# Sixty one-number memsets on VectorE ahead of gamma's copy, in a grouped instance norm

## The chip, the cores and the metric

The kernel runs on one core of one Trainium2 chip. The metric is the device time of one execution, in microseconds (us). Before the change three runs gave 626.84, 627.01 and 627.31 us, a median of 627.01 us.

## The reference

x has the shape 4 x 8 x 16 x 256 x 256 in float32, 134 MB; gamma has 8 x 16 numbers. Each of the 512 channels (4 x 8 x 16) is normed over its 65,536 pixels and multiplied by its gamma:

```python
mu = x.mean(axis=(3, 4), keepdims=True)
var = ((x - mu) ** 2).mean(axis=(3, 4), keepdims=True)
x_norm = (x - mu) / np.sqrt(var + 1e-5)
out = x_norm * gamma[None, :, :, None, None]
```

So 134 MB are read and 134 MB are written.

## The kernel before

A unit is 16 channels. Each channel is spread over S = 8 partitions, so a unit is a tile of 128 partitions x 8192 numbers, 4.19 MB, and there are U = 32 units. Six slots (AHEAD = 6) hold units; unit u uses slot u % 6 and is normed in place.

The order of the work is the order in which the program is written, engine by engine (the schedule is manual): each engine goes through its own instructions in order, and waits for another engine or for a transfer only where the data demand it.

*Setup.* VectorE clears a small tile, touch (L53). POOL's queue then writes touch over 16 short stretches of the first unit's output (L54), which the first unit's store later overwrites, and loads gamma into g_row, one row of 128 numbers (L55). The first six units are loaded at once, units 1 and 3 from ScalarE's queue, the others from SP's (the helper at L48). POOL makes eps_t, one and navg, a 128 x 128 matrix that holds -1/65536 where two partitions belong to one channel (L61 to L70). VectorE waits for gamma and copies it into g_rep with each number repeated 8 times (L81); TensorE turns the row into columns with one small matmul for each of the 8 groups of 16 channels (L86), and VectorE copies the result to g_col (L92).

*The loop over 32 units.* VectorE sums the tile (L105) while ScalarE squares and sums it (L106). TensorE adds these sums over the 8 partitions of each channel (L114). VectorE makes the negative variance (L115), ScalarE the root (L119), VectorE the reciprocal (L123) and its product with g_col (L125), then VectorE norms the tile in place (L128). ScalarE's queue stores it (L132), and SP's queue loads unit u + 6 into the same slot (L48), once that store has landed.

Three things set the order around the change. VectorE's first instructions are touch's memset, gamma's copy, g_col's copy and the first reduction, in that order. POOL's first transfer waits for touch's memset. Gamma's copy waits for gamma's transfer.

Of the kernel before, what the change touches and what calls it, by code (L numbers as in the profile page):

```python
# [1 line left out]

# [4 lines left out]

F32 = mybir.dt.float32
U8 = mybir.dt.uint8
ALU = mybir.AluOpType  # L10
ACTF = mybir.ActivationFunctionType
AX = mybir.AxisListType


@with_exitstack
def kernel(
    ctx: ExitStack,
    tc: tile.TileContext,
    x: bass.AP,
    gamma: bass.AP,  # L20
    out: bass.AP,
):
    nc = tc.nc
    B, G, C, H, W = x.shape
    P = nc.NUM_PARTITIONS
    HW = H * W
    n_ch = B * G * C
    S = 8
    K = P // S
    F = HW // S  # L30
    U = n_ch // K
    NG = (G * C) // K
    AHEAD = 6
    assert HW % S == 0 and (G * C) % K == 0

    xv = x.rearrange("b g c h w -> (b g c h w)").rearrange("(u p f) -> u p f", p=P, f=F)
    ov = out.rearrange("b g c h w -> (b g c h w)").rearrange("(u p f) -> u p f", p=P, f=F)
    gv = gamma.rearrange("g c -> (g c)")

    data = ctx.enter_context(tc.tile_pool(name="data", bufs=1))  # L40
    singles = ctx.enter_context(tc.tile_pool(name="singles", bufs=1))
    psum = ctx.enter_context(tc.tile_pool(name="psum", bufs=4, space=bass.MemoryType.PSUM))
    ctx.enter_context(tc.manual_schedule())

    slots = [data.tile([P, F], F32, name=f"xt{i}") for i in range(AHEAD)]

    def load(u, queue):
        queue.dma_start(out=slots[u % AHEAD][:], in_=xv[u])  # L48


    g_row = singles.tile([1, G * C], F32, name="g_row")
    touch = singles.tile([16, 128], F32, name="touch")
    nc.vector.memset(touch[:], 0.0)  # L53
    nc.gpsimd.dma_start(out=ov[0][0::S, 0:128], in_=touch[:])  # L54
    nc.gpsimd.dma_start(out=g_row[:], in_=gv[None, :])  # L55
    for u in range(AHEAD):
        load(u, nc.scalar if u in (1, 3) else nc.sync)


    eps_t = singles.tile([P, 1], F32, name="eps_t")  # L60
    nc.gpsimd.memset(eps_t[:], 1e-5)  # L61
    one = singles.tile([1, 1], F32, name="one")
    nc.gpsimd.memset(one[:], 1.0)
    navg = singles.tile([P, K, S], F32, name="navg")
    nc.gpsimd.memset(navg[:], -1.0 / HW)  # L65
    nc.gpsimd.affine_select(  # L66
        out=navg[:], in_=navg[:], pattern=[[-S, K], [0, S]], compare_op=ALU.is_ge,
        fill=0.0, base=0, channel_multiplier=1,
    )
    nc.gpsimd.affine_select(  # L70
        out=navg[:], in_=navg[:], pattern=[[S, K], [0, S]], compare_op=ALU.is_ge,
        fill=0.0, base=S - 1, channel_multiplier=-1,
    )
    navg_w = navg[:].rearrange("p k s -> p (k s)")
    root_eps = singles.tile([P, 1], F32, name="root_eps")
    nc.scalar.activation(out=root_eps[:], in_=eps_t[:], func=ACTF.Sqrt)  # L76
    g_rep = singles.tile([1, NG, K, S], F32, name="g_rep")
    g_ps = psum.tile([P, NG], F32, name="g_ps", bufs=1)
    g_col = singles.tile([P, NG], F32, name="g_col")

    nc.vector.tensor_copy(  # L81
        out=g_rep[:],
        in_=g_row[:].rearrange("o (n k) -> o n k", n=NG).unsqueeze(3).to_broadcast([1, NG, K, S]),
    )
    for n in range(NG):
        nc.tensor.matmul(  # L86
            out=g_ps[:, n : n + 1],
            lhsT=g_rep[:, n].rearrange("o k s -> o (k s)"),
            rhs=one[:],
            start=True, stop=True,  # L90
        )
    nc.vector.tensor_copy(out=g_col[:], in_=g_ps[:])  # L92

    junk = singles.tile([P, F], U8, name="junk")

    st = singles.tile([P, U, 2], F32, name="st")
    nvar = singles.tile([P, U], F32, name="nvar")
    std = singles.tile([P, U], F32, name="std")
    rstd = singles.tile([P, U], F32, name="rstd")
    scale = singles.tile([P, U], F32, name="scale")  # L100

    squares = []
    for u in range(U):
        t = slots[u % AHEAD]
        nc.vector.reduce_sum(out=st[:, u, 0:1], in_=t[:], axis=AX.X)  # L105
        square = nc.scalar.activation(  # L106
            out=junk[:], in_=t[:], func=ACTF.Square, accum_out=st[:, u, 1:2],
        )
        if u:

            tc.declare_no_dep(square.ins, squares[-1].ins, reason="junk, ordered by the root between")
        squares.append(square)
        ps = psum.tile([P, 2], F32, name="ps")
        nc.tensor.matmul(out=ps[:], lhsT=navg_w, rhs=st[:, u], start=True, stop=True)  # L114
        nc.vector.tensor_scalar(  # L115
            out=nvar[:, u : u + 1], in0=ps[:, 0:1], scalar1=ps[:, 0:1],
            scalar2=ps[:, 1:2], op0=ALU.mult, op1=ALU.add,
        )
        nc.scalar.activation(  # L119
            out=std[:, u : u + 1], in_=nvar[:, u : u + 1], func=ACTF.Sqrt,  # L120
            bias=eps_t[:], scale=-1.0,
        )
        nc.vector.reciprocal(out=rstd[:, u : u + 1], in_=std[:, u : u + 1])  # L123
        g = u % NG
        nc.vector.tensor_mul(  # L125
            out=scale[:, u : u + 1], in0=rstd[:, u : u + 1], in1=g_col[:, g : g + 1],
        )
        nc.vector.tensor_scalar(  # L128
            out=t[:], in0=t[:], scalar1=ps[:, 0:1], scalar2=scale[:, u : u + 1],
            op0=ALU.add, op1=ALU.mult,  # L130
        )
        nc.scalar.dma_start(out=ov[u], in_=t[:])  # L132
        if u + AHEAD < U:
            load(u + AHEAD, nc.sync)


# [1 line left out]
_INS = ['x', 'gamma']  # L138
_OUTS = [((4, 8, 16, 256, 256), 'float32')]


# [23 lines left out]
```

## Time and profile before

| what | value |
|---|---|
| median of three runs | 627.01 us |
| span of the profiled execution, first to last instruction | 625.4 us |
| median less span | 1.6 us |
| bytes moved by DMA | 268.46 MB, mean 429 GB/s |
| VectorE (DVE) busy | 443.4 us, 71% of the span |
| ScalarE (ACT) busy | 238.8 us, 38% |
| granted TensorE clock | 1.000 |
| touch's transfer, issue to landing | 9.1 us |
| gamma's transfer, issue to landing | 13.3 us |
| a load of x on SP's queue, median, issue to landing | 38.5 us |
| a store, median, issue to landing | 62.5 us |

The profile is of one execution; it gives its span and no other time of it, so the median of the unprofiled runs is set beside the span. Engines appear as PE (TensorE matmul), PEld (its weight loads), DVE (VectorE), ACT (ScalarE), POOL (GpSimd) and SP; a q behind the name is the engine's queue, which waits and issues DMAs. A group of instructions has the line, the engine, the operation, out<-in, the shapes and the count, then the busy time in us and the mean of one in ns, then the idle time of the engine just before and what ended it. The slices are 40 equal parts of the span (15.6 us each), a digit is the busy share in tenths, and GB/s is what the DMA engines moved. A load or store takes long from issue to landing where it stands in a queue with others.

### The profile page before, as it was taken

To read this page: it belongs to the slowest core of one execution; us is meant where nothing else is said; L and a number is where in the kernel's file an instruction comes from. 1 tells how busy PE (TensorE), PEld (TensorE's weight loads), DVE (VectorE), ACT (ScalarE), POOL (GpSimd) and SP (SyncE) were. 2 spreads that over 40 slices of the span, in tenths; PEclk is the share of its full clock that TensorE was granted. 3 is DMA by queue.
4 is the path that set the end of the run, shared out by engine and by line. 5 is a ranking of instruction groups with operands and counts; after the bars stand their busy time and mean duration, and the time that the engine had idled before them with its cause. 6 is when DMAs were issued, how large, how long until landed. Compare 5 with 4: busy or idle time off the path is not lost.

```text
span 625.4 us, 631 instructions
## 1 busy us (share of the span) xinstructions
PE 21.4 (3%) x80; PEld 19.5 (3%) x80; DVE 443.4 (71%) x163; ACT 238.8 (38%) x98; POOL 2.4 (0%) x11
## 2 busy tenths in 40 slices
PE   0200000000000000000000000000000000000000
PEld 0200000000000000000000000000000000000000
DVE  0588999999776687666776767867668676686730
ACT  0444444444443244432344423444224442244400
POOL 1000000000000000000000000000000000000000
DMA  8999999999999999999999999999999999999998
GB/s 369 436 402 436 436 436 436 436 434 424 434 436 432 432 428 434 436 436 436 436 434 423 434 436 432 436 428 434 434 436 436 436 436 432 425 434 434 434 432 363
DMA packets 9282, 268.46 MB, mean 429 GB/s; under 512 B 1072, under 2 KB 1088, under 8 KB 1088
## 3 DMA queue, kind: packets, MB, share of 16 engines
q10 hardware_dynamic: 4896, 142.61, 52.9%
q1 hardware_dynamic: 4320, 125.83, 46.7%
q0 software_dynamic: 64, 0.01, 0.0%
q14 instruction: 2, 0.02, 0.0%
HBM read 134.22 MB, written 134.23 MB: 429 GB/s over the span
## 4 chain that ended last, share of the span: by engine, by line
another core or an unknown queue 61%; DMA 17%; DVE 15%; SPq 1%; PE 1%; issue 0%; ACT 0%
DVE st L105 10%; DMA xt<-in_x_dram 10%; DMA out_dram<-xt 8%; DVE xt L128 5%; SPq L48 1%; PE ps L114 1%; ACT std L119 0%; DVE nvar L115 0%; DVE rstd L123 0%; DVE scale L125 0%
## 5 line engine op out<-in xcount | busy, mean ns | idle before, releaser
L105 DVE TENSOR_REDUCE st<-xt 128x1 f32<-128x8192 f32 x32 | 277.9, 8685 | 100.8 <-DMA xt<-in_x_dram 100.8
L106 ACT ACTIVATE junk<-xt 128x8192 uint8<-128x8192 f32 x32 | 225.0, 7030 | 275.6 <-DMA xt<-in_x_dram 232.4
L128 DVE TENSOR_SCALAR xt<-xt,ps,scale 128x8192 f32<-128x8192 f32 x32 | 145.6, 4551 | 1.2
L119 ACT ACTIVATE std<-nvar,eps_t 128x1 f32<-128x1 f32 x32 | 9.4, 295 | 79.6 <-DVE nvar L115 79.6
L114 PE MATMUL ps<-st,navg 128*128 128x2 f32 x64 | 17.8, 348 | 557.6 <-DVE st L105 557.6
L114 PEld LDWEIGHTS ps<-st,navg 128*128 128x128 f32 x64 | 16.0, 311 | 559.4 <-issue 559.4
L115 DVE TENSOR_SCALAR nvar<-ps 128x1 f32<-128x1 f32 x32 | 9.2, 288 | 23.8 <-PE ps L114 23.8
L123 DVE RECIPROCAL rstd<-std 128x1 f32<-128x1 f32 x32 | 5.3, 164 | 11.6 <-ACT std L119 11.6
L81 DVE COPY g_rep<-g_row 1x1024 f32<-1x1024 f32 x1 | 0.7, 681 | 14.2 <-DMA g_row<-in_gamma_dram 14.2
L106 ACT ACTIVATION_READ_ACCUMULATOR junk<-xt 128x1 f32 x32 | 6.0, 187 | 0.0
L125 DVE TENSOR_TENSOR scale<-rstd,g_col 128x1 f32<-128x1 f32 x32 | 5.1, 160 | 1.1
L86 PE MATMUL g_ps<-one,g_rep 1*128 1x1 f32 x16 | 3.5, 347 | 16.1 <-DVE g_rep L81 16.1
L86 PEld LDWEIGHTS g_ps<-one,g_rep 1*128 1x128 f32 x16 | 3.5, 326 | 16.1 <-issue 16.1
L92 DVE COPY g_col<-g_ps 128x8 f32<-128x8 f32 x1 | 0.2, 167 | 3.7 <-PE g_ps L86 3.7
L76 ACT ACT_TABLE_LOAD x1 | 1.3, 1283 | 1.7 <-PEq L149 1.7
L53 DVE MEMSET touch<- 16x128 f32 x1 | 0.2, 165 | 0.9 <-PEq L149 0.9
L54 POOL DMA_DIRECT2D out_dram<-touch x1 | 0.6, 617 | 0.8 <-DVE touch L53 0.8
L55 POOL DMA_DIRECT2D g_row<-in_gamma_dram x1 | 0.5, 484 | 0.0
L66 POOL TENSOR_SCALAR_AFFINE_SELECT navg<-navg 128x128 f32<-128x128 f32 x1 | 0.4, 398 | 0.1
L70 POOL TENSOR_SCALAR_AFFINE_SELECT navg<-navg 128x128 f32<-128x128 f32 x1 | 0.4, 397 | 0.1
L65 POOL MEMSET navg<- 128x128 f32 x1 | 0.2, 231 | 0.0
L76 ACT ACTIVATE root_eps<-eps_t 128x1 f32<-128x1 f32 x1 | 0.2, 203 | 0.0
(6 smaller groups left out, 0.6 us busy)
## 6 DMA issues: line engine op xcount, KB each, us to landing
out_dram<-xt ACTq DMA_DIRECT2D x32, 4096.0 KB, 62.5
xt<-in_x_dram SPq DMA_DIRECT2D x30, 4096.0 KB, 38.5
xt<-in_x_dram ACTq DMA_DIRECT2D x2, 4096.0 KB, 31.7
out_dram<-touch POOLq DMA_DIRECT2D x1, 8.0 KB, 9.1
g_row<-in_gamma_dram POOLq DMA_DIRECT2D x1, 0.5 KB, 13.3
```

Source lines behind the costliest of these rows:

```text
L48: queue.dma_start(out=slots[u % AHEAD][:], in_=xv[u])
L76: nc.scalar.activation(out=root_eps[:], in_=eps_t[:], func=ACTF.Sqrt)
L81: nc.vector.tensor_copy(out=g_rep[:], in_=g_row[:].rearrange("o (n k) -> o n k", n=NG).unsqueeze(3).to_broadcast([1, NG, K, S]),)
L86: nc.tensor.matmul(out=g_ps[:, n : n + 1], lhsT=g_rep[:, n].rearrange("o k s -> o (k s)"), rhs=one[:], start=True, stop=True,)
L105: nc.vector.reduce_sum(out=st[:, u, 0:1], in_=t[:], axis=AX.X)
L106: square = nc.scalar.activation(out=junk[:], in_=t[:], func=ACTF.Square, accum_out=st[:, u, 1:2],)
L114: nc.tensor.matmul(out=ps[:], lhsT=navg_w, rhs=st[:, u], start=True, stop=True)
L115: nc.vector.tensor_scalar(out=nvar[:, u : u + 1], in0=ps[:, 0:1], scalar1=ps[:, 0:1], scalar2=ps[:, 1:2], op0=ALU.mult, op1=ALU.add,)
L119: nc.scalar.activation(out=std[:, u : u + 1], in_=nvar[:, u : u + 1], func=ACTF.Sqrt, bias=eps_t[:], scale=-1.0,)
L123: nc.vector.reciprocal(out=rstd[:, u : u + 1], in_=std[:, u : u + 1])
L125: nc.vector.tensor_mul(out=scale[:, u : u + 1], in0=rstd[:, u : u + 1], in1=g_col[:, g : g + 1],)
L128: nc.vector.tensor_scalar(out=t[:], in0=t[:], scalar1=ps[:, 0:1], scalar2=scale[:, u : u + 1], op0=ALU.add, op1=ALU.mult,)
```

## The change

Behind the issue of the first six loads in the program's text, a new tile of 64 numbers on one partition is made, and VectorE clears its first 60 numbers one by one. Nothing reads the tile. On VectorE these instructions come behind touch's memset and ahead of gamma's copy.

```diff
     for u in range(AHEAD):
         load(u, nc.scalar if u in (1, 3) else nc.sync)
 
+    spare = singles.tile([1, 64], F32, name="spare")
+    for i in range(60):
+        nc.vector.memset(spare[:, i : i + 1], 0.0)
 
     eps_t = singles.tile([P, 1], F32, name="eps_t")
     nc.gpsimd.memset(eps_t[:], 1e-5)
```

## The prediction

> **What bounds the kernel now.** I read the page from the top: the busy shares first, then the slices, because a share is only a mean. VectorE (DVE) has the largest share, yet the two last lines of the slices carry the verdict.
>
> ```profile
> PE 21.4 (3%) x80; PEld 19.5 (3%) x80; DVE 443.4 (71%) x163; ACT 238.8 (38%) x98; POOL 2.4 (0%) x11
> ...
> DVE  0588999999776687666776767867668676686730
> ...
> DMA  8999999999999999999999999999999999999998
> GB/s 369 436 402 436 436 436 436 436 434 424 434 436 432 432 428 434 436 436 436 436 434 423 434 436 432 436 428 434 434 436 436 436 436 432 425 434 434 434 432 363
> ...
> q14 instruction: 2, 0.02, 0.0%
> ...
> L105 DVE TENSOR_REDUCE st<-xt 128x1 f32<-128x8192 f32 x32 | 277.9, 8685 | 100.8 <-DMA xt<-in_x_dram 100.8
> ```
>
> The DMA row is at 8 or 9 tenths from the first slice to the last, and the rate hardly leaves 436 GB/s. The table of stretches gives 433 GB/s between 100 and 500 us. At that rate the page's 268.46 MB take 268.46 / 0.433 = 620.0 us of a span of 625.4. So the DMA engines bound the kernel, and only a change that lets them run dry, or adds bytes, can move the end by much. VectorE stands idle for 100.8 us in front of its reductions, in wait for loads: it is the faster partner in the steady part.
>
> Next the start, in the timeline of instructions (start, duration, engine, line, in brackets the idle time before).
>
> ```profile
> 0.34 0.10 POOL L149 MEMSET const-float32-1.0<- 128x1 f32 x1
> 0.38 0.10 POOL L149 MEMSET const-bfloat16-1.0<- 128x1 bf16 x1
> ...
> 0.89 0.17 DVE L53 MEMSET touch<- 16x128 f32 x1 [0.89 <-PEq L149]
> 1.36 0.62 POOL L54 DMA_DIRECT2D out_dram<-touch  x1 [0.85 <-DVE touch L53]
> ...
> 1.98 0.48 POOL L55 DMA_DIRECT2D g_row<-in_gamma_dram  x1
> ...
> 15.29 0.68 DVE L81 COPY g_rep<-g_row 1x1024 f32<-1x1024 f32 x1 [14.23 <-DMA g_row<-in_gamma_dram]
> ...
> 19.70 0.17 DVE L92 COPY g_col<-g_ps 128x8 f32<-128x8 f32 x1 [3.73 <-PE g_ps L86]
> ...
> 22.57 8.69 DVE L105 TENSOR_REDUCE st<-xt 128x1 f32<-128x8192 f32 x1 [2.71 <-DMA xt<-in_x_dram]
> ...
> 33.05 4.55 DVE L128 TENSOR_SCALAR xt<-xt,ps,scale 128x8192 f32<-128x8192 f32 x1
> 37.51 8.68 DVE L105 TENSOR_REDUCE st<-xt 128x1 f32<-128x8192 f32 x1
> 37.63 0.35 ACTq L132 DMA_DIRECT2D out_dram<-xt  x1
> ```
>
> The place of the change is the 14.23 us between touch's memset (ends at 1.06) and gamma's copy at 15.29. VectorE does nothing there; it waits for gamma's transfer. Behind it lies a second reserve: g_col is ready at 19.87 (19.70 + 0.17), and the first reduction starts only at 22.57, when the first unit of x has landed, 2.71 us later. The chain that ended last agrees: its first piece is that load, from 0.81 to 22.55, and neither gamma nor touch is in it.
>
> Last the end, in the waits of SP's queue (total us, times, longest us).
>
> ```profile
> SPq L160 <- DMA out_dram<-xt: 38.4, 4, 9.6
> ```
>
> After the last load SP waits for four stores one behind the other, 38.4 / 4 = 9.6 us each. A store of 4.19 MB at 433 GB/s is 9.7 us. The last store is issued at 600.80 and lands 23.6 us later: 14 us of that it stands behind stores issued before it. The end is a draining queue, and compute could be some 14 us later there at no cost.
>
> **The change, step by step.** Nothing is removed. 60 memsets of one number each are added to VectorE, behind touch's memset (L53) and ahead of gamma's copy (L81). The tile is new and nobody reads it, so no engine waits for them; touch's memset stays first, and POOL's transfer at L54, which waits for it, is released as before. No DMA is added or moved on any queue.
>
> *The pace of a memset.* No row shows such a memset, so I bound it. From below: POOL's small memsets start 0.03 us apart (0.34, 0.38) though each lasts 0.10; 60 x 0.03 = 1.8 us. From above: each memset waits for the end of the one before, if the framework orders writes to one tile. The row for that is the reciprocal at 32.65 and the multiplication behind it at 32.85, which needs its result: 0.20 us from start to start; 60 x 0.20 = 12.0 us. I take a value between: VectorE's own memset of a wider tile lasts 0.165 us, and two independent VectorE instructions overlap by 0.09 us (the one at 33.05 ends at 37.60, the next begins at 37.51), which leaves 0.075 us a piece, 4.5 us in all.
>
> The sum: 1.06 + 4.5 = 5.6 us, and at the upper end 1.06 + 12.0 = 13.1 us. Both are ahead of 15.29, so gamma's copy starts when it did, and the cost is nothing. The cover is gamma's transfer; it is gone from (15.29 - 1.06) / 60 = 0.237 us a memset. Beyond that the 2.71 us in front of the first reduction still hide the delay, up to (14.23 + 2.71) / 60 = 0.282 us.
>
> The Trainium skill, Perfetto Trace Analysis, section Optimizing Scalar/DVE Operations, gives about 60 ns of engine time for a VectorE access to SBUF, and a profiled length of about twice that. By it 60 memsets would be an estimated 3.6 us, and the sum would be the same nothing.
>
> *POOL beside them.* POOL writes touch's and gamma's descriptors from 1.36 to 2.46, now beside the memsets. From below that costs nothing, and it can gain nothing, since the first of them still waits for touch's memset. From above, the memsets shut POOL out until the last has ended, at 13.1: touch's issue moves from 1.36 to 13.1, 11.7 us, and gamma's copy with it to 27.0. g_col ends 4.58 us after the copy starts (19.87 - 15.29), so at 31.6; the first reduction, queued behind it on VectorE, starts 31.6 - 22.57 = 9.0 us late, and the first store at 46.6 instead of 37.63. I take nothing, since POOL's row of 0.62 us for the issue and VectorE's one-partition write of four bytes show no reason for more.
>
> A rule speaks against this change: the Trainium skill, SBUF — State Buffer, section SBUF: two separate sides, warns that a DMA issued from GpSimd is held up while VectorE runs an operation in a mode that uses two ports. Its section Who interferes with whom says that a VectorE instruction with at most one SBUF input outside those modes does not contend. No run here shows either; by the first the sum would hold a late gamma, by the second nothing.
>
> *Code.* 60 more instructions have to be loaded. The page shows two instruction packets in the whole span, 0.02 MB; the trace has them at 156 and 200 us, 8 KB and 0.31 us each. One more would cost one of the 16 DMA engines 0.31 us. Whether VectorE would stop for it, no row shows. From above I take gamma's transfer, also small and also among the loads: 13.3 us from issue to landing. With the dearest memsets, VectorE would then reach the copy at 1.06 + 12.0 + 13.3 = 26.4, and the first store would be 26.4 + 4.58 - 22.57 = 8.4 us late, at 46.0. I take 0 and keep 0.31 us for the range.
>
> *What a late first store costs.* This is the step that makes the upper ends harmless. Six loads are issued at once, 25.17 MB, 58.1 us at 433 GB/s. The first two land at 22.5, and they are 19.4 us of transfer, so the stream begins at 3.1 and lasts to 61.2 without any store. The first store adds 9.7 us: 70.9. When it lands, SP issues the seventh load; the second store follows the first by 14.9 us, VectorE's period (37.51 - 22.57). So the engines run dry only if the second store is issued later than 70.9, which puts the first later than 56.0, that is over 18.4 us late. Both upper ends above, 46.6 and 46.0, are well short of that. In the steady part VectorE needs 14.9 us a unit and the transfers 8.39 MB / 0.433 = 19.4 us, so a lateness of 9 us is made up within three units.
>
> The sum of the change against the profiled span is therefore 625.4 + 0 = 625.4 us. The median of the runs, 627.01, lies 1.6 us above that span; the change has no part in that rest, so the forecast is 627.0 us.
>
> **The rivals.**
>
> *The first store moves, the end hardly.* POOL held up or a stop for code, as above, with the first store 8 to 9 us late. For it: small transfers among the loads take 13.3 us here. Against it: the writes are tiny and the cover is 14 us. The bytes stay the same, only the mixing of loads and stores changes. Between 36 and 48 us, where the first store meets the loads, the stretches show 401, 385 and 393 GB/s: (3 x 433 - 1179) x 4 / 433 = 1.1 us lost. This could be lost again or saved: 625.9 to 628.1 us, within 0.2% at both ends.
>
> *Slower.* The memsets hold up VectorE so long that the engines run dry. Place: between the loads' end at 61.2 and the seventh load. It decides from a first store 18.4 us late, which takes (22.57 + 18.4 - 4.58 - 1.06) / 60 = 0.59 us a memset. The only short hop in the profile that dear is from VectorE through PE and back, 0.74 us idle ahead of L115. At that price the first store starts 1.06 + 44.4 + 4.58 - 22.57 = 27.5 us late, at 65.1; the engines stand 3.9 us after 61.2, and once more for the restart, which by the table of stretches lost about 2.3 us between 0 and 6 us of the span. That is 6.2 us: 633.2 us. Against it: these memsets wait for no other engine.
>
> *The change does not do what it says.* The memsets might be dropped or merged on the way to the chip, since nobody reads them. The time would be 627.0 us as well; only the profile could tell it from the forecast.
>
> **How the numbers follow.** The forecast, memsets hidden under gamma's transfer, 0.88; the memsets not there, 0.01; the first store late, 0.06; slower through a dry queue, 0.03; the remaining 0.02 is for a gain that I can't name. A difference of 0.2% (1.25 us) is about what a measurement of this kernel can tell from no change. Within it: 0.88 + 0.01 + 0.05 of the late store = 0.94. Slower: 0.03 + 0.01 of the late store = 0.04. Faster: 0.02. The range: the three runs of before reach from 626.84 to 627.31, 0.47 wide; as much again on each side is 626.37 to 627.78, and 0.31 for one instruction packet makes the upper end 628.1. So 626.3 to 628.1 us, which also takes in the upper half of the late store.
>
> **What would show it right or wrong.** Right: 60 memsets between 1.06 and at most 13.1 us, copy of g_rep at about 15.3 with a wait for gamma still ahead of it (some 10 us), first reduction at about 22.6, first store at about 37.6, slices as before. A copy at 27 with POOL's issues late says that POOL was shut out; memsets with a hole in their row say code. If the first store is in its place and the time still moves by over 1.25 us, the reasoning from the queues is wrong.

## The result and the profile after

The changed kernel took 629.72 us (median of 7 runs, 628.17 to 631.45) beside 626.87 us before: a ratio of 1.0045, 95% interval 1.0033 to 1.0057. It is slower by 2.8 us and outside the range of the prediction. Repeated three times later it had ratios of 1.0028 to 1.0030, and medians 1.4 to 1.7 us above those of before, again outside the range. The profiled execution has a span of 626.6 us instead of 625.4.

The page of the changed kernel, slices, queues and the new group:

```profile
DVE  1598999999776687666786767857678676686730
...
DMA  8999999999999999999999999999999999999997
GB/s 369 433 416 433 423 435 435 435 435 435 435 435 436 427 429 431 435 435 431 435 435 435 425 435 435 436 433 435 435 435 433 429 427 431 435 435 435 435 435 326
...
q14 instruction: 3, 0.02, 0.0%
...
L61 DVE MEMSET spare<- 1x1 f32 x60 | 1.6, 59 | 0.0
```

The mean rate is as high as before in the middle and lower in the last slice, 326 GB/s instead of 363. There is one more instruction packet. The memsets take 1.6 us together.

The start in its timeline (start, duration, engine, line, idle time before):

```profile
1.00 1.61 DVE L61 MEMSET spare<- 1x1 f32 x60
1.36 0.62 POOL L54 DMA_DIRECT2D out_dram<-touch  x1 [0.85 <-DVE touch L53]
...
1.97 0.48 POOL L55 DMA_DIRECT2D g_row<-in_gamma_dram  x1
...
16.07 0.68 DVE L84 COPY g_rep<-g_row 1x1024 f32<-1x1024 f32 x1 [13.46 <-DMA g_row<-in_gamma_dram]
...
23.36 8.69 DVE L108 TENSOR_REDUCE st<-xt 128x1 f32<-128x8192 f32 x1 [2.72 <-DMA xt<-in_x_dram]
...
38.42 0.35 ACTq L135 DMA_DIRECT2D out_dram<-xt  x1
```

The memsets end at 2.61, and VectorE then still waits 13.46 us for gamma: the cover is as wide as predicted. POOL issues its two transfers when it did. Yet gamma, the first load and the first store are all 0.8 us late. The time of the memsets is not the reason; the transfers themselves take longer (touch's 9.8 us from issue to landing instead of 9.1, gamma's 14.1 instead of 13.3).

Where the end moved is seen in the table of stretches, between 624.00 and 625.20 us (length, busy time of each engine, clock, DMA share, GB/s), of the kernel before:

```profile
624.00:625.20 1.20, 0.00 (x0) 0.00 (x0) 0.00 (x0) 0.00 (x0) 0.00 (x0) 1.00 0.00 0
```

and of the changed kernel:

```profile
624.00:625.20 1.20, 0.00 (x0) 0.00 (x0) 0.00 (x0) 0.00 (x0) 0.00 (x0) 1.00 0.06 27
```

A share of 0.06 is one of 16 engines, and 27 GB/s over 1.2 us is one packet of 32,768 bytes; a packet is counted where it begins. Before, none begins in this stretch, and the last one ends at 624.10. After, fifteen engines are done by then and one moves its last packet of the last store until 625.29. The difference of the spans, 1.2 us, is that packet.

**Reading the lag.** The DMA records of the trace do not name the engine. But each load or store ends with 16 tiny packets, one from each engine, so the lateness of the last against the median tells how far the slowest engine is behind at that moment. Before, the slowest ends 0.58 us behind a median of 623.53. After, it ends 1.80 us behind a median of 623.49; 1.80 - 0.58 - 0.04 = 1.18 us, the whole change of the span. The lag of the changed kernel grows in steps: 0.87 at the landing of the first load (22 us; before 0.15), 1.36 when the second pair of transfers ends at 42 us (before 0.40), slowly back to 0.97 until 391 us, then 1.82 at 410 us, and 1.80 at the end. The records put packets of 8192 bytes of code at 7.5, 199 and 407 us; before they were at 156 and 200. The view of the DMA queues has one such packet in each of these stretches, 7 to 8 and 406 to 407.2 us of the changed kernel and 155 to 157 of the kernel before (packets, MB, share of the 16 engines):

```profile
q14 instruction: 1, 0.01, 1.9%
q14 instruction: 1, 0.01, 1.6%
q14 instruction: 1, 0.01, 1.0%
```

The steps up at 22 and 410 us are those of the packets at 7.5 and 407, and the step of before, 0.30 to 0.64 at 158 us, is its packet at 156; that step is smaller because the packet met an engine that was 0.30 us ahead of the slowest. Such a packet lasts 0.31 us, and the data packet behind the one at 7.5 took 1.72 us instead of 1.213: 0.31 + 0.51 = 0.82 us a crossing. The packet at 199 us makes no step, so it took another engine. The records bear this out without a name: an engine begins its next packet within 20 ns of the end of the one before, so 16 chains of packets can be followed through the trace. In the changed kernel the packets at 7.5 and 407 us lie on one chain, the one that ends last (the second begins at 406.608, where that chain's data packet ends at 406.611), and the packet at 199 on another. In r3_forty below, the first and the last packet lie on one chain in the same way.

### The profile page after: what moved, and what is told of

Same layout as the page of the kernel before. It is cut to its first block, busy times and chain, and to the rows that moved or that the text cites. A ratio compares the mean times of both kernels' runs of the same rounds, so it can differ in the third digit from the quotient of the medians.

```text
span 626.6 us, 691 instructions
## 1 busy us (share of the span) xinstructions
PE 21.4 (3%) x80; PEld 19.5 (3%) x80; DVE 444.9 (71%) x223; ACT 238.8 (38%) x98; POOL 2.4 (0%) x11
## 4 chain that ended last, share of the span: by engine, by line
another core or an unknown queue 61%; DMA 17%; DVE 15%; SPq 1%; PE 1%; issue 0%; ACT 0%
DMA xt<-in_x_dram 10%; DVE st L108 10%; DMA out_dram<-xt 8%; DVE xt L131 5%; SPq L48 1%; PE ps L117 1%; ACT std L122 0%; DVE nvar L118 0%; DVE rstd L126 0%; DVE scale L128 0%
## 5 line engine op out<-in xcount | busy, mean ns | idle before, releaser
L84 DVE COPY g_rep<-g_row 1x1024 f32<-1x1024 f32 x1 | 0.7, 681 | 13.5 <-DMA g_row<-in_gamma_dram 13.5
L61 DVE MEMSET spare<- 1x1 f32 x60 | 1.6, 59 | 0.0
## 6 DMA issues: line engine op xcount, KB each, us to landing
g_row<-in_gamma_dram POOLq DMA_DIRECT2D x1, 0.5 KB, 14.1
```

The lines of the kernel that those rows point to most:

```text
L61: nc.vector.memset(spare[:, i : i + 1], 0.0)
```

## The experiments

**The theory after this: code pages.** VectorE's program of 169 instructions (the page counts 163; it leaves out 6 that only wait or drain) became one of 229. It crosses a boundary of its code in the setup instead of in the loop, and one boundary more. Each crossing loads 8 KB through one DMA engine, the same one each time, which falls some 0.85 us behind; and since all transfers use all 16 engines and the queues never empty, it does not catch up, and the last store waits for it. **Rivals:** the 0.8 us of the late start are carried to the end; the new tile moves addresses; the memsets themselves, by their time or their number.

In the table, lag 41 is that of the slowest engine behind the median at 41 to 42 us, when the first store meets the loads, lag end at the last store. Times are medians; before was at 626.9 to 627.1 beside each.

| kernel | code packets at, us | lag 41 | lag end | span | us | ratio and interval |
|---|---|---|---|---|---|---|
| before | 156, 200 | 0.40 | 0.58 | 625.4 | 626.87 | |
| change | 7.5, 199, 407 | 1.36 | 1.80 | 626.6 | 629.72 | 1.0045 (1.0033 to 1.0057) |
| r1_same | 7.5, 199, 407 | 2.04 | 2.09 | 626.7 | 628.62 | 1.0030 (1.0019 to 1.0041) |
| r8_same | 7.4, 199, 406 | 1.41 | 1.49 | 626.4 | 628.43 | 1.0028 (1.0017 to 1.0040) |
| r11_same | 7.6, 202, 407 | 2.28 | 2.39 | 626.9 | 628.63 | 1.0029 (1.0019 to 1.0039) |
| r2_one | 144, 199 | 0.36 | 1.11 | 625.8 | 627.18 | 1.0004 (0.9995 to 1.0013) |
| r3_forty | 37, 199, 485 | 2.26 | 2.45 | 627.1 | 628.43 | 1.0024 (1.0014 to 1.0034) |
| r4_behind | 24, 199, 407 | 2.04 | 2.09 | 626.7 | 628.77 | 1.0028 (1.0017 to 1.0039) |
| r6_pool | 9.7, 156, 199 | 0.20 | 1.02 | 625.7 | 627.11 | 1.0007 (0.9996 to 1.0017) |
| r7_unit9 | 156, 199, 407 | 0.32 | 1.84 | 626.6 | 627.75 | 1.0013 (1.0005 to 1.0022) |
| r9_110 | 7.5, 199, 213 | 1.75 | 2.92 | 627.7 | 629.05 | 1.0030 (1.0018 to 1.0042) |
| r10_many9 | 156, 183, 200, 426 | 0.59 | 2.22 | 627.0 | 628.74 | 1.0027 (1.0016 to 1.0038) |
| r5_many | 7.6, 13, 207, 452 | 2.20 | 12.6 | 652.8 | 661.13 | 1.0409 (1.0389 to 1.0429) |
| r12_many_gcol | 27, 33, 212, 456 | 1.86 | 12.6 | 666.5 | 670.86 | 1.0707 (1.0689 to 1.0725) |

**r1_same: the change again.**

> The changed kernel once more, for its spread and a second trace. Pages theory: VectorE's longer program crosses a boundary of its code at its 50th instruction and again some 125 later, and each crossing fetches a packet of 8 KB that holds up one of the 16 DMA engines by 0.8 us (0.31 for itself, 0.5 in the packet behind it); the end waits for the slowest engine. It expects 3 instruction packets in the span, the first near 7 us, and 628 to 631 us, the time depending on which engines the packets fall on. Late-start theory: the first load, gamma and the first store are each 0.8 us late and everything behind them with it; it expects 0.8 us over before, 627.7 us, each time.

Three packets, the first at 7.5 us, a slowest engine 2.09 us behind, 628.62 us (628.09 to 629.45). The late-start theory wanted 627.7 each time; its loss is too small, and the next runs take it away altogether.

**r2_one: the same numbers cleared by one instruction.**

```diff
-    for i in range(60):
-        nc.vector.memset(spare[:, i : i + 1], 0.0)
+    nc.vector.memset(spare[:, 0:60], 0.0)
```

> The 60 memsets become one memset over the same 60 numbers; the new tile stays. Pages theory: 2 packets as before, the first near 155 us, and the time of before, 626.9 us. If the new tile (it moves the addresses of the tiles behind it) or a write into it were the cause: the time of the change, 628 to 631 us.

627.18 us, no difference that the interval shows. The tile, its address and the write cost nothing; the 59 instructions do. The page has the two packets of before:

```profile
q14 instruction: 2, 0.02, 0.0%
```

**r3_forty: 40 memsets, with range(40).**

> 40 memsets in the same place. VectorE's 50th instruction is then in the third unit of the loop. Pages theory, by the number of packets: still 3 in the span, the first near 50 us instead of 7, the last near 470 us; 627.5 to 631 us, the loss stays. Pages theory, by the place of the first: a packet in the first 10 us is what costs, so the time of before, 626.9 us. Late-start theory: the first load lands as before (22.6 us), so 626.9 us. If the memsets' own time on VectorE were the cause, two thirds of the loss: about 628.8 us.

The loss stays, 1.5 us, with a packet at 37 us. The first load lands as in before, so neither the late start nor a packet in the first 10 us is needed, and 40 memsets cost as much as 60 did in the repeats.

**r4_behind: the 60 memsets behind g_col's copy.**

```diff
     nc.vector.tensor_copy(out=g_col[:], in_=g_ps[:])
+    spare = singles.tile([1, 64], F32, name="spare")
+    for i in range(60):
+        nc.vector.memset(spare[:, i : i + 1], 0.0)
```

> The same 60 memsets behind g_col's copy instead of ahead of gamma's. Pages theory: 3 packets, the first near 24 us, the last near 407 us, and a loss like that of the change, 628 to 631 us. Late-start theory: the first load lands as before at 22.6 us but the first reduction stands behind 1.6 us of memsets, of which 2.7 us of waiting hide all; 626.9 us. A hold-up of POOL's transfers by the memsets: POOL is done by then, so 626.9 us.

628.77 us. POOL and gamma are done when these memsets run, and the loss is the same.

**r6_pool: the 60 memsets on POOL, behind its setup.**

```diff
+    spare = singles.tile([1, 64], F32, name="spare")
+    for i in range(60):
+        nc.gpsimd.memset(spare[:, i : i + 1], 0.0)
     navg_w = navg[:].rearrange("p k s -> p (k s)")
```

> The 60 memsets go to POOL, behind its last setup instruction; VectorE has the program of before. Pages theory: POOL crosses a boundary too, 3 packets in the span, VectorE's at 156 us again. If all processors' packets take the same DMA engine: the loss of the change, 628.6 us. If POOL's take another one than VectorE's: two engines are late by one packet each and not one by two, 627.2 to 627.8 us. Rival, it is something in VectorE's memsets or in its code alone: 626.9 us.

627.11 us, and no loss that the interval shows, though there are three packets, one at 9.7 us among the loads. No engine stands out after POOL's packet (0.28 us at 22 us, 0.20 at 41): it lasted 0.31 us and slowed one data packet by 0.21, on an engine that was not behind. The slowest falls back with VectorE's packet at 156 (1.22 at 158 us). The time alone would also fit the rival, something in VectorE's code alone (626.9); the trace shows why the third packet is free. So the number of packets in the span is not what counts, but which engine takes them.

**r7_unit9: the 60 memsets in the loop, behind the norming of unit 9.**

```diff
+    spare = singles.tile([1, 64], F32, name="spare")
...
+        if u == 9:
+            for i in range(60):
+                nc.vector.memset(spare[:, i : i + 1], 0.0)
         nc.scalar.dma_start(out=ov[u], in_=t[:])
```

> The same 60 memsets on VectorE, but in the loop, behind the norming of unit 9 (VectorE waits 4.3 us for the next load there). VectorE's first crossing is then near 156 us as before, the second near 407 us as in the change: 3 packets. Pages theory: the slowest engine ends about 0.85 us later than before, 627.6 to 628 us; the rest of the change's loss (the packet in the load phase, where the lag grows once more at 40 us when the first store meets the loads) is not there. Rival, only an early packet costs: 626.9 us. Rival, only the number of packets counts: 628.6 us.

627.75 us, as the pages theory had it, in two groups (627.55 to 627.79, and 628.29 to 628.47, with the profiled run among the latter). The packets at 156 and 407 us show as steps of 0.38 to 1.36 and of 0.99 to 1.84. By the medians the same three packets thus cost 0.7 us without one in the load phase, and 1.4 to 1.7 us with one. Why is not shown. With an early packet of VectorE's the lag grows again at the first store, from 0.91 at 22 us to 2.04 at 41 in r1_same and from 0.96 to 2.28 in r11_same, where kernels without one stay at 0.59 or less; but at 391 us these two are back at 1.27 and 1.58, the change is at 0.97 and r8_same at 0.64, beside 0.99 here. And the traced run of r7_unit9 ends as far behind, 1.84 us, as the change's, 1.80.

**r8_same and r11_same: the change twice more.**

> The changed kernel a third time, since its runs went from 628.1 to 631.5 us so far. Pages theory: slowest of the 16 DMA engines about 2 us behind the median one at the end, 628 to 629.5 us; if a run near 631 us is profiled, its slowest engine is over 4 us behind, or else the theory lacks a part.

> The changed kernel once more, for a profile of one of its runs near 631 us, of which there were 4 in 21. Pages theory: 628 to 629.5 us with a slowest engine some 2 us behind; in a run near 631 us an engine over 4 us behind.

628.43 and 628.63 us. One run of r8_same took 631.05 us, beside three of the first seven of the change and one of r6_pool's twelve (631.12); no run of before did. None of these was the profiled one, so what they hold stays open, and with it the difference between the first ratio of 1.0045 and the repeats' 1.0028 to 1.0030.

**r5_many: 185 memsets ahead of gamma's copy, with range(185) and a tile of 192.**

> 185 memsets in place of 60 (the tile is widened to 192 numbers). Pages theory: VectorE crosses a boundary at its 50th, 175th and 300th instruction, so 4 packets in the span (near 7, 10 to 15, 199 and 407 us); the one engine that takes VectorE's packets falls behind by some 0.85 us more than in the change, 0.6 + 3 x 0.85 or a little over, and the end is about 629.5 us. If VectorE has to stop for its next page, a hole of some us shows in the row of memsets, and gamma's wait still hides it. Rival, the number of instructions alone counts (each memset costs the end the same): 3.1 times the loss of the change, 632 us. Rival, an early packet counts once: 628.6 us, as the change.

661.13 us, against an expected 629.5: the sum of packets is refuted for this kernel, and the rival's 632 too. The memsets are hidden here as well; in the timeline they pause once, for 0.37 us, and gamma's copy still waits 10.6 us:

```profile
1.01 1.61 DVE L61 MEMSET spare<- 1x1 f32 x60
...
2.98 3.56 DVE L61 MEMSET spare<- 1x1 f32 x125 [0.37 <-issue]
...
17.14 0.68 DVE L84 COPY g_rep<-g_row 1x1024 f32<-1x1024 f32 x1 [10.60 <-DMA g_row<-in_gamma_dram]
```

The pause is the boundary itself: ahead of it stand 63 instructions (touch's memset, 60 of the new ones, and two that the view leaves out). It is no wait for the packets: VectorE goes on at 2.98 us, and the packets move at 7.6 and 13.3. The damage is in the transfers. The table of stretches of this kernel:

```profile
44.00:200.00 156.00, 5.58 (x20) 5.02 (x20) 132.56 (x50) 70.06 (x30) 0.00 (x0) 1.00 1.00 425
200.00:400.00 200.00, 5.02 (x18) 4.51 (x18) 131.41 (x47) 72.89 (x28) 0.00 (x0) 1.00 1.01 423
```

and of the kernel before:

```profile
44.00:200.00 156.00, 5.58 (x20) 5.01 (x20) 132.77 (x51) 69.62 (x31) 0.00 (x0) 1.00 1.00 433
200.00:400.00 200.00, 5.58 (x20) 5.01 (x20) 144.96 (x51) 79.89 (x32) 0.00 (x0) 1.00 1.00 433
```

The engines are always busy (1.00 and 1.01) and move 425 and 423 GB/s instead of 433: packets take longer. From 44 to 400 us a load's packet took 32 to 49 ns over its 1.213 us on the mean, at most 2 ns before. Over the whole run that is 8.7 us an engine (631.4 us of data packets on the mean engine, 622.7 before), of the 27.4 us by which this run's span grew. The larger part lies in engines that no longer end together. The slowest engine goes from 2.2 us behind at 41 us to 13.5 at 380, and the queue ends ragged, in the page's last slices:

```profile
GB/s 383 420 412 444 422 422 424 418 430 424 428 428 420 422 418 430 428 422 416 424 410 436 430 416 424 428 414 430 434 434 434 434 434 434 434 432 436 422 253 58
```

**r9_110: 110 memsets, with range(110) and a tile of 128.**

> 110 memsets in place of 60, same place. The 185 memsets cost 34 us, not the 2.5 us that a sum of packets gives; this kernel has 50 instructions more than the change but, with 279 on VectorE, no further boundary (50, 175, not 300). Pages theory: 3 packets, the first near 7 us, VectorE's second one near 215 us instead of 407; 628 to 629.5 us, like the change. Rival, each memset costs, and more so the more there are: the loss lies between that of 60 and that of 185, 635 us or more.

629.05 us. 50 more memsets than the change, and no more boundaries, cost 0.4 to 0.6 us over the repeats; nothing like the 34 us. The number of instructions alone is not what counts. One thing here does not fit a lag that only packets move: without a packet on VectorE's account after 213 us, the slowest engine creeps from 2.34 us behind at 217 us to 4.11 at 565, and is back at 2.92 at 585. The cause is open.

**r10_many9: the 185 memsets behind the norming of unit 9, the edit of r7_unit9 with range(185) and a tile of 192.**

> The 185 memsets behind the norming of unit 9 instead of ahead of gamma's copy: 4 packets, VectorE's second and third within some 6 us of each other near 180 us, when loads and stores already alternate. Theory A, the 34 us come from one engine that is 2 us late or more, whenever that happens (its packets then collide with those of the others all through the rest): some 10 to 30 us lost here too. Theory B, they come from two packets on one engine during the first loads, ahead of the first store: here only the sum of the packets, 0.6 + 3 x 0.85 us behind the median engine, 628.5 to 629.5 us.

628.74 us, inside the 628.5 to 629.5 of theory B, with a lag of 2.22 us at the end instead of 3.15: four packets, and no more than their sum is lost. Against theory A, an engine that is 2.22 us late from 429 us on slows nothing down here. It is a weaker test of B than I had meant: VectorE read ahead and fetched its first page at 156 us already, so its two packets are 28 us apart and not 6. Its row of memsets has the same pause, 0.36 us, 128 instructions later: 55 stand ahead of the memsets, and 55 + 136 = 191 = 63 + 128.

```profile
174.63 3.22 DVE L135 MEMSET spare<- 1x1 f32 x136
...
178.22 1.42 DVE L135 MEMSET spare<- 1x1 f32 x49 [0.36 <-issue]
```

At the end one engine is again alone in the table of stretches:

```profile
624.00:625.20 1.20, 0.00 (x0) 0.00 (x0) 0.00 (x0) 0.00 (x0) 0.00 (x0) 1.00 0.06 27
```

**r12_many_gcol: the 185 memsets behind g_col's copy.**

> The 185 memsets behind g_col's copy: VectorE's first two packets fall near 24 and 30 us, after touch's and gamma's transfers and still ahead of the first store. They end near 25.5 us instead of 19.9, so the first reduction is some 2.5 us late, which by itself costs the end nothing. If it is two packets on one engine during the loads, ahead of the first store, that cost the 185 memsets 34 us: 640 us or more here too. If it is what they do to touch's and gamma's transfers in the first 15 us: 629 to 630 us, the sum of the packets.

670.86 us. Touch and gamma are untouched here (the copy starts at 15.32), so what was done to them is not the cause. What r5_many and r12_many_gcol share, and no other kernel has, is two packets of VectorE's within 6 us among the first loads; in r5_many both lie on one chain. That these packets cost the 34 to 44 us, and not the 185 memsets in the load phase by some other way, is argued: r9_110 with 110 of them there lost 2.1 us. Whether the same pair would do it later in the run was not tried. Why it does is not settled: at 41 us its slowest engine is 1.86 us behind, no more than the 2.04 of r4_behind, which lost 1.9 us, so the lag at that point does not tell the two apart.

## Why the prediction was wrong, step by step

*What bounds the kernel: right, but read too coarsely.* The DMA engines bound it. I treated them as one pool of 433 GB/s that only a dry queue or more bytes can delay. They are 16 engines, each with a fixed sixteenth of every transfer, 512 data packets of 1.213 us, and the end is that of the slowest. Before, fifteen of them end within 0.64 us of one another and one 0.47 us after these. What reaches one engine is not shared out: the data packets took 622.7 us on the mean engine before and 622.8 after, and the end moved by 1.18 us.

*The pace of a memset: harmless.* The memsets start 0.027 us apart (1.61 / 60) and last 59 ns each, a little below my lower bound of 0.03 and a third of the 0.075 that I took. No framework wait stands between them. The 60 ns of engine time in the Trainium skill (Perfetto Trace Analysis, Optimizing Scalar/DVE Operations) is here the length of one, and not the distance between two.

*POOL beside them: right.* Its issues at 1.36 and 1.97 last 0.62 and 0.48 us as before; the memsets did not hold it up. Of the two places of the Trainium skill that I weighed (SBUF — State Buffer), the trace agrees with Who interferes with whom; the hold-up of the other, for modes that use two ports, did not occur, and whether a memset can run in such a mode no run here shows.

*Code: the step that failed.* I wrote that one more packet would cost one of the 16 engines 0.31 us, took nothing, and kept 0.31 us for the range. That there would be one more was right. Three things were not. A packet of VectorE's sets its engine back by 0.8 to 1.0 us and not 0.31, since the data packet behind it is slowed as well. VectorE's packets add up on one engine, 0.87 at the first and 0.85 at the last here, and the end pays the sum. And the crossing of before was not added to but moved, from 156 to 7.5 us, into the load phase, where by the medians it cost 0.7 to 0.9 us more (r7_unit9 lost 0.7, the repeats 1.4 to 1.7). The packet more is shown by its step; the price of the move rests on the medians alone. The first measurement's 629.72 us lies 1.1 to 1.3 above the repeats, and that rest stays open. The sign I had named for code, a hole in the row of memsets, did not come: the row is one piece (x60), and the code cost all the same.

The Trainium skill (Runtime: NRT & Kernel Launch, Instruction fetch mechanics) has code refilled in blocks of 16 KiB, 256 instructions, and the boundary mostly hidden. The runs differ: packets of 8 KB, boundaries 128 instructions apart, and a boundary that VectorE hardly feels (0.37 us, hidden) but the end does.

*A late first store: right in itself.* It came 0.8 us late, short of the 18.4 us at which I had the engines run dry, and r3_forty has the same loss with a first load in time. No queue ran dry. *The rivals:* none of them held the cause; the slower one had the wrong mechanism. I argued that 60 memsets are hidden, which they are, and so gave 0.94 to no change.

Nothing here beats the kernel before: by its own trace only 0.47 us (0.58 less the 0.11 of the second slowest engine) lie in the slowest engine, less than these measurements tell apart.

## What to carry to other kernels

Where the DMA queues are full from start to end, count instructions as traffic: an engine's program is loaded in pages, each page passes through one DMA engine, and most of that engine's lag stays until the last store (1.36 us at 42 us and 0.97 at 391 in the change). Look at the last microseconds in a table of stretches: a share of 0.06 there is one engine in 16 that everybody waits for. And do not let a setup run through page boundaries while the first loads are in flight; by the medians the same instructions cost half as much in the loop, and as one instruction nothing that could be measured.

## What the runs showed of the hardware that I had not expected

- A packet of 8 KB of code lasts 0.31 us (309 ns; 325 for the second of two within 6 us), and sets its DMA engine back by 0.8 to 1.0 us (VectorE's; POOL's one by some 0.5).
- VectorE's 63rd and 191st instruction are followed by a pause of 0.36 to 0.39 us when it runs without waits; the packets come some 13 to 16 instructions earlier when it waits in between (156 us in before, 407 in the change).
- The lag of one engine grows further when the first store meets the loads (0.87 to 1.36 us in the change, 0.96 to 2.28 in r11_same), and part of it is gone by 391 us (0.97 and 1.58).
- The two kernels with two code packets within 6 us during the first loads lost 34 and 44 us; in r5_many the transfers ran at 423 to 425 instead of 433 GB/s from 44 to 400 us, and the engines ended far apart. How the one leads to the other is open.
